# The first layer's gated outputs are stored through GpSimd's DMA queue instead of SyncE's

## The chip, the cores and the metric

The kernel runs on one core of a Trainium2 chip. The metric is the device time of one execution in microseconds (us), taken as the median of several runs. The engines are named as the profile names them: PE is TensorE's matmul side and PEld its weight loads, DVE is VectorE, ACT is ScalarE, POOL is GpSimd, SP is SyncE. SP computes nothing here; it only issues DMAs, one after the other, in the order of its instruction stream. SPq and POOLq are the queues of DMA issues of those engines.

## The reference, cut to what is computed

The program is one inference step of a decoder with two layers, on a prompt of 2048 positions and on a sample group of 8 sequences with 4 positions each, with the same weights. The width is 1024. The first layer is gated linear attention, with 4 heads of key width 128 and value width 512:

```python
def gla_mixer(h, state0, norm_g, w_in, w_gate2, b_gate, out_norm_g, w_out):
    u = rmsnorm(h, norm_g)
    q, k, v, gate, g_low = split(u @ w_in)
    log_a = log_sigmoid(g_low @ w_gate2 + b_gate) / 16
    o, state = gla_recurrence(q * 128 ** -0.5, k, v, log_a, state0)
    o = rmsnorm(o, out_norm_g)
    return (o * silu(gate)) @ w_out, state
```

The recurrence keeps a 128 x 512 state for each head; within a chunk, position t reads position s with a weight that decays channel by channel with the summed log_a between them. After the first layer, keys and values are projected once from the normalised residual. The second layer is attention over a window of 128 positions with sinks, with a gate path of the same kind, that reads those keys and values. The kernel returns the residual streams, the states and the last keys and values.

## The kernel before

All large matrix products run on PE in float16. Each float32 operand is split into a high and a low half, and each product is made in three passes (high by high, and two mixed ones), so PE has three times the matmuls that plain float16 would need. The helper `split` (lines 189 to 198) makes the two halves: the high half is a copy on ACT (line 194, or 197 with a scale), the low half a subtraction on POOL or DVE (line 195, or 198 with a scale).

**The first layer.** For each of the 4 heads the kernel walks over 4 blocks of 512 positions, and in each block over 4 chunks of 128. A block first projects q, k, the log gates, v and the gate path (matmuls into the PSUM tile `pj`, whose inputs are the weights `W` and the transposed, normalised input `uT`). It then makes the decayed scores by levels (lines 500 to 536): for each level POOL (line 508) and DVE (line 509) form differences of summed logs in the tile `E`, ACT takes the exponential, DVE multiplies by k and q, `split` writes both halves into the tile `X` (2 buffers), PE multiplies into `lev`, and DVE copies what belongs to this level into the score tile `S`. A chunk (lines 562 to 616) is a list of steps: `kv` (state update product), `out` (readout into `o`), `upd` (the new state and its halves), `norm` (ACT squares and sums, POOL takes the power in lines 186 and 187, DVE multiplies the readout by the norm and the gate into the tile `og`, 1 buffer), and last `spill_og`.

**The touched step.** `spill_og` (lines 620 to 623) takes a buffer of `ogT` (128 x 2 x 512 float16, 2 buffers), splits `og` into it, high half on ACT (line 194), low half on POOL (line 195), and stores it to the DRAM tensor `ogd` with one DMA of 256 KB (line 623). The trace has 68 of these stores. They are read back much later, when the output projection of the first layer runs. `ogT` also carries the normalised input of each 128 positions until it is transposed: `norm_T` (lines 300 to 322) uses `og` as scratch for the squares (lines 302 and 307), writes the halves into `ogT` (lines 197 and 198), and SP issues the transposing DMAs to `uT` (line 322).

**What else SP and POOL do there.** SP loads the inputs (line 382), the constants (line 108), the raw weights, the rope tables (line 894 into the tile `pst`, 2 buffers) and issues the transposing DMA of `ke` (line 558). POOL multiplies the rope tables by the norm's gains (lines 897, or 899 and 900), stores them (line 901, its own DMA queue, tensor `rtd`), and later prepares the weights of the next products: `prepare` splits them into `pst` and stores them from POOL's queue (line 248, tensor `pre`, 72 stores).

**What sets the order.** The program is written as lists of steps with priorities (`behind`), woven together. A scheduler then fixes the order of instructions on each engine, from a timeline of its own at build time. So a changed instruction can move others. On the chip each engine runs its stream in order, and waits on semaphores where an operand or a buffer is not ready. An instruction that waits holds up all that stands behind it on its engine; that includes DMA issues on SP and on POOL.

Of the kernel before, what the change touches and what calls it, by code (L numbers as in the profile page):

```python
# [74 lines left out]
def _body(tc, nc, cp, sb, ps, dr, i, o):  # L75
# [6 lines left out]
    def T(tag, shape, dt, bufs=None):  # L82
        return sb.tile(shape, dt, tag=tag, name=nm(tag), **({} if bufs is None else {"bufs": bufs}))
# [106 lines left out]
    def split(dst, src, sc=None, eng=dve):  # L190

        hi, lo = dst
        if sc is None:
            act(hi, src, AF.Copy)  # L194
            eng.tensor_tensor(lo, src, hi, ALU.subtract)  # L195
        else:
            act(hi, src, AF.Copy, scale=sc)  # L197
            dve.scalar_tensor_tensor(lo, src, sc, hi, ALU.mult, ALU.subtract)  # L198
# [217 lines left out]
    class Blk:  # L416
# [149 lines left out]
        def chunk_steps(self, c):  # L566
# [40 lines left out]
            def norm():  # L607
# [6 lines left out]
                dve.scalar_tensor_tensor(og, po, r[:, 0:1], self.sg[c], ALU.mult, ALU.mult)  # L614

            return behind([kv, out, upd, norm], -20) + [lambda: spill_og(box["og"], ogd[j * 4 + c], h, pool)]

    state = [None]

    def spill_og(og, dst, h, eng):  # L620
        ot = T("ogT", [P, 2, 512], F16, 2)
        split((ot[:, 0], ot[:, 1]), og, eng=eng)
        nc.sync.dma_start(dst[:, :, h * 512 : (h + 1) * 512], ot)

    def spill_halves(og, c, g):

# [1217 lines left out]
```

## Time and profile before

| what | value |
|---|---|
| median of 3 runs | 2862.65 us |
| the three runs | 2855.01, 2862.65, 2867.41 us |
| the profiled execution's own time | 2863.85 us |
| its span (first to last instruction) | 2862.1 us |
| mean granted clock of PE over the span | 0.983 |
| PE busy | 2735.9 us, 96% of the span |
| DVE, ACT, POOL busy | 1845.7, 1440.3, 1063.6 us |

The profiled execution took 1.75 us more than its span, and 1.2 us more than the median of the runs. The first layer's blocks run from about 100 us to 1180 us: the 68 stores of line 623 begin at 106.5 us and end at 1160.2 us. Before that lie the first loads and the first transposes, behind it the output projection of the first layer, the shared keys and values, and the second layer. Busy time of an engine counts instructions that compute; an issue of a DMA has a duration in the trace too, but is not counted as busy.

### The profile page before, as it was taken

How to read it: one execution, taken by the hardware profiler on the slowest of the kernel's cores; microseconds unless marked ns; L12 is line 12 of the kernel's file. 1: busy time of each engine (PE TensorE's matmuls, PEld its weight loads, DVE VectorE, ACT ScalarE, POOL GpSimd, SP SyncE). 2: the span in 40 equal slices, each digit the busy share in tenths (PEclk: the TensorE clock that was granted, in tenths of full speed). 3: DMA queues.
4: the chain of work that ended last, by engine and by line, in shares of the span. 5: the costliest groups of instructions: out<-in, count | busy, mean ns of one | idle time of the engine just before them, and what ended most of it. 6: DMA issues, size and time to landing. Idle time of an engine off the chain costs nothing.

```text
span 2862.1 us, 51609 instructions
## 1 busy us (share of the span) xinstructions
PE 2735.9 (96%) x19070; PEld 1392.4 (49%) x19070; DVE 1845.7 (64%) x3815; ACT 1440.3 (50%) x3385; POOL 1063.6 (37%) x1471
## 2 busy tenths in 40 slices
PE   6899999999999999999899999999999999988999
PEld 3445444444454444444344555555555555543444
DVE  5767787677768775336413666677777766767653
ACT  6655665466546654333313555566666666641110
POOL 1242233222322321116405676666566556530000
PEclk9899999999999999999999999999999999999999
DMA  8351334124312533799975555866877788798651
GB/s 209 90 124 36 100 101 150 38 82 136 115 38 85 171 84 96 180 240 282 233 193 135 108 130 120 203 117 129 173 116 130 157 155 165 151 236 172 125 112 57
DMA packets 774230, 391.78 MB, mean 137 GB/s; under 512 B 629200, under 2 KB 698776, under 8 KB 773944
## 3 DMA queue, kind: packets, MB, share of 16 engines
q1 hardware_dynamic: 761016, 352.75, 54.6%
q0 software_dynamic: 10880, 35.66, 3.4%
q8 instruction: 149, 2.44, 0.4%
q14 instruction: 105, 0.86, 0.1%
q10 hardware_dynamic: 2080, 0.07, 0.0%
HBM read 138.90 MB, written 107.54 MB: 86 GB/s over the span
## 4 chain that ended last, share of the span: by engine, by line
PE 56%; DVE 12%; DMA 11%; ACT 10%; issue 6%; POOL 4%; SPq 1%; DVEq 0%; ACTq 0%; POOLq 0%
PE pj L101 33%; PE o L101 11%; PE tr L101 8%; PE kv L101 3%; ACT o L1279 2%; DMA pst<-v 2%; DVE v L198 2%; ACT v L197 2%; DMA pre<-pst 1%; PE lev L101 1%; DMA wraw<-in_a_w_in_dram 1%; DVE o L1274 1%; DVE W L198 1%; POOL ogT L195 1%; DVE lev L1274 1%
## 5 line engine op out<-in xcount | busy, mean ns | idle before, releaser
L101 PE MATMUL pj<-W,uT 128*128 128x512 f16 x5088 | 1208.1, 383 | 6.6 <-ACT qT L430 2.9
L101 PEld LDWEIGHTS <-uT 128*128 128x128 f16 x6976 | 654.7, 99 | 714.1 <-issue 40.4
L101 PE MATMUL tr<-W,uT 128*128 128x512 f16 x1536 | 365.8, 379 | 0.0
L186 POOL TENSOR_SCALAR rs_m<-ss 128x1 f32<-128x1 f32 (+3 forms) x190 | 46.1, 243 | 685.7 <-ACT og L611 234.0
L101 PEld LDWEIGHTS <-X 128*128 128x128 f16 x2744 | 185.8, 98 | 149.3 <-issue 14.7
L1279 ACT ACTIVATE o<-o,mx 128x256 f32<-128x256 f32 (+1 forms) x384 | 168.5, 439 | 168.1 <-DVE mx L1274 163.6
L1274 DVE CUSTOM_DVE_ANT_0 o<-o,madd,nsink 128x256 f32<-128x256 f32 (+1 forms) x384 | 184.0, 479 | 48.3 <-PE o L101 44.0
L101 PE MATMUL pj<-uT,W 128*128 128x512 f16 (+1 forms) x912 | 186.0, 354 | 27.0 <-DMA uT<-ogT 24.3
L198 DVE SCALAR_TENSOR_TENSOR v<-o,v 128x512 f16<-128x512 f32 (+1 forms) x192 | 128.8, 671 | 102.0 <-ACT v L197 82.0
L187 POOL TENSOR_TENSOR rs_r<-rs_m,mhalf 128x1 f32<-128x1 f32 (+2 forms) x186 | 184.8, 994 | 14.4
L101 PEld LDWEIGHTS <-W 128*128 128x128 f16 x2448 | 128.0, 98 | 113.1 <-issue 18.5
L101 PEld LDWEIGHTS <-v 128*128 128x128 f16 x976 | 95.2, 98 | 116.0 <-DMA v<-ogd 1.9
L508 POOL TENSOR_TENSOR E<-bt 128x256 f32<-128x256 f32 x96 | 73.9, 770 | 198.4 <-DVE X L195 124.8
L195 POOL TENSOR_TENSOR ogT<-og,ogT 128x512 f16<-128x512 f32 x68 | 88.0, 1295 | 154.4 <-ACT ogT L194 142.5
L101 PEld LDWEIGHTS <-sth 128*128 128x128 f16 x2080 | 111.4, 99 | 52.3 <-DMA sth<-v 12.2
L101 PEld LDWEIGHTS <-sg 128*128 128x128 f16 x800 | 78.6, 99 | 107.5 <-DMA sg<-ogd 12.3
L101 PE MATMUL o<-gl,X 128*128 128x256 f16 (+1 forms) x768 | 114.9, 273 | 5.5 <-DMA X<-qe 5.5
L197 ACT ACTIVATE v<-o 128x512 f16<-128x512 f32 (+1 forms) x192 | 111.3, 579 | 11.1 <-DMA sth<-v 7.6
L101 PE MATMUL kv<-rmask,sth 128*128 128x64 f16 x1984 | 107.0, 194 | 10.1 <-DMA sth<-v 9.2
L101 PE MATMUL kv<-rmask,pst 128*128 128x64 f16 x992 | 102.4, 194 | 9.3 <-DMA pst<-v 9.3
L1279 ACT ACTIVATE lev<-lev,mx 128x256 f32<-128x256 f32 (+1 forms) x128 | 56.5, 441 | 103.3 <-DVE mx L1274 101.2
L101 PE MATMUL pj<-W,v 128*128 128x512 f16 x448 | 104.2, 379 | 1.1 <-DMA v<-ogd 1.1
(468 smaller groups left out, 5092.5 us busy)
## 6 DMA issues: line engine op xcount, KB each, us to landing
pre<-pst POOLq DMA_DIRECT2D x72, 256.0 KB, 3.4
W<-pre SPq DMA_DIRECT2D x36, 512.0 KB
ogd<-ogT SPq DMA_DIRECT2D x68, 256.0 KB
wraw<-in_a_w_in_dram SPq DMA_DIRECT2D x64, 256.0 KB
wraw<-in_b_w_in_dram SPq DMA_DIRECT2D x64, 256.0 KB
oge<-ogT SPq DMA_DIRECT2D x64, 256.0 KB
wraw<-in_a_w_out_dram SPq DMA_DIRECT2D x32, 256.0 KB
X<-in_x_prompt_dram SPq DMA_DIRECT2D x32, 256.0 KB
```

Of the source, the lines that this page charges most:

```text
L101: return order(nc.tensor.matmul(*a, **k))
L186: pool.tensor_scalar(m[:n, :k], ss, a, b, ALU.mult, ALU.add)
L187: pool.tensor_tensor(r[:n, :k], m[:n, :k], mhalf[:n, :k], ALU.pow)
L195: eng.tensor_tensor(lo, src, hi, ALU.subtract)
L197: act(hi, src, AF.Copy, scale=sc)
L198: dve.scalar_tensor_tensor(lo, src, sc, hi, ALU.mult, ALU.subtract)
L508: pool.tensor_tensor(Ev[:, :, 0, :], ref, btv[:, :, 0, :], ALU.subtract)
L1274: dve.tensor_tensor_reduce(pm[:, z], pm[:, z], madd.rearrange("p a b -> p (a b)")[:, (2 - nk) * P :], -0.125, nsink[:, g * GRP + h : g * G ...
L1279: act(pm[:, z], pm[:, z], AF.Exp, scale=-1.0, bias=nm_[:, h : h + 1], accum_out=bx["sum"][:, h : h + 1])
```

## The change

One line changes: the store at the end of `spill_og` is issued by GpSimd's queue.

```diff
     def spill_og(og, dst, h, eng):
         ot = T("ogT", [P, 2, 512], F16, 2)
         split((ot[:, 0], ot[:, 1]), og, eng=eng)
-        nc.sync.dma_start(dst[:, :, h * 512 : (h + 1) * 512], ot)
+        nc.gpsimd.dma_start(dst[:, :, h * 512 : (h + 1) * 512], ot)
```

Over the program SP's stream loses 68 rows (1448 to 1380) and POOL's gains 68 (1469 to 1537). On POOL each store stands directly behind the subtraction of line 195 that fills its buffer, at some places with one small instruction between. The scheduler also reorders neighbours in the first layer. PE, DVE and ACT keep the same instructions; on PE the order differs at places up to about a third of the stream, and is the same from there to the end.

On SP, in the stretch in which the constants of line 108 are loaded (from about 137 us in the trace of before), one stretch of the difference reads as follows; `W_1974` is a piece of the input, `ogd_99` the store of one chunk, `gso` and `gskv` are the first two of the constants.

```order
 L322 DMA_TRANSPOSE uT_158<-ogT_1460 128x8x128
 L322 DMA_TRANSPOSE uT_158<-ogT_1461 128x8x128
-L382 DMA W_1974<-in_x_prompt_dram 128x512 x2
-L623 DMA ogd_99<-ogT_1513 256x1x512
 L108 DMA gso<-in_a_out_norm_dram 128x4x1
 L108 DMA gskv<-in_kv_norm_dram 128x8x1
```

The constants follow directly on the transposes; the load of `W_1974` stands further down now, between two of the last constants (`bmq` and `smask`), and another store (`ogd_100`) that stood ahead of the first rope load is gone from SP as well.

On POOL, at the rope tables (from about 159 us in the trace of before), where `pst_2857` and `pst_2865` are the third and fourth table, `rtd` their stores, and `ogT_1860` the buffer of the chunk whose store is `ogd_101`, the difference reads:

```order
-L901 DMA rtd<-pst_2673 128x8x64
-L195 TENSOR_TENSOR ogT_1860<-og_1849,ogT_1860 128x512
 L899 TENSOR_TENSOR pst_2857<-pst_2857,gq 128x8x32
 L900 TENSOR_TENSOR pst_2857<-pst_2857,gq 128x8x32
+L899 TENSOR_TENSOR pst_2865<-pst_2865,gq 128x8x32
+L900 TENSOR_TENSOR pst_2865<-pst_2865,gq 128x8x32
+L195 TENSOR_TENSOR ogT_1860<-og_1849,ogT_1860 128x512
+L901 DMA rtd<-pst_2857 128x8x64
+L901 DMA rtd<-pst_2865 128x8x64
+L623 DMA ogd_101<-ogT_1860 256x1x512
 L186 TENSOR_SCALAR rs_m_1959<-ss_1955 128x1
```

The subtraction that fills `ogT_1860` stood ahead of the third table's multiplications and now stands behind those of the third and fourth; its store comes after the two stores of the tables.

On PE, a little later (at about 179 us in the trace of before), the first product of a block's diagonal level, `lev_1879`, stands among the projections `pj_2050` of another block. In the difference its surroundings read:

```order
+L101 MATMUL pj_2050<-W_701,uT_157 128x512
+L101 LDWEIGHTS uT_157
+L101 MATMUL pj_2050<-W_701,uT_157 128x512
 L101 LDWEIGHTS X_1876
 L101 MATMUL lev_1879<-one_h,X_1876 128x1
 L101 LDWEIGHTS uT_157
-L101 MATMUL pj_2050<-W_692,uT_157 128x512
-L101 LDWEIGHTS uT_157
-L101 MATMUL pj_2050<-W_692,uT_157 128x512
```

Nine of the projection matmuls that stood behind `lev_1879` now stand ahead of it. Elsewhere on PE the level products move ahead of at most 8 such matmuls.

## Rows read from the trace of the kernel before

**Rows 1.** Page, part 1: busy us, share of the span, instructions of each engine

```profile
PE 2735.9 (96%) x19070; PEld 1392.4 (49%) x19070; DVE 1845.7 (64%) x3815; ACT 1440.3 (50%) x3385; POOL 1063.6 (37%) x1471
```

**Rows 2.** Windows: stretch, length, busy PE, PEld, DVE, ACT, POOL, clock, DMA share, GB/s

```profile
140.00:230.00 90.00, 83.17 (x468) 39.39 (x467) 63.34 (x115) 53.05 (x103) 34.84 (x48) 0.97 0.49 118
230.00:1180.00 950.00, 927.40 (x5887) 446.99 (x5886) 682.06 (x1217) 540.84 (x1004) 240.83 (x355) 0.99 0.33 99
```

**Rows 3.** Waits of SP's queue, whole span: total us, times, longest us

```profile
SPq L623 <- POOL ogT L195: 262.0, 40, 22.1
```

**Rows 4.** Waits of PE: first two lines 100 to 230 us, others 230 to 1180

```profile
PE pj L101 <- DMA uT<-ogT: 1.7, 1, 1.7
...
PE kv L101 <- DMA ke<-X: 0.8, 1, 0.8
...
PE lev L101 <- ACT ssm L194: 5.8, 3, 2.5
PE kv L101 <- ACT v L197: 4.6, 4, 1.8
PE kv L101 <- DVE v L198: 3.9, 4, 2.4
...
PE o L101 <- DVE ke L774: 0.5, 1, 0.5
```

**Rows 5.** Line 623: ns min/median/max of an issue, first and last start

```profile
L623 SPq DMA_DIRECT2D ogd<-ogT x68: 533/546/1201, 106.5 to 1160.2; - x68
```

**Rows 6.** Line 248 on POOL, the same view, and its landing times

```profile
L248 POOL DMA_DIRECT2D pre<-pst x72: 677/690/785, 414.0 to 1283.8; - x72
...
DMA to landing us min/median/max: 2.5/3.4/6.1
```

**Rows 7.** Timeline of POOL behind line 195: start us, us, instruction, [idle before <- releaser]

```profile
107.75 0.61 POOL L508 TENSOR_TENSOR E<-bt 128x256 f32<-128x256 f32 x1 [1.30 <-DVE X L195]
...
140.42 0.18 POOL L544 COPY ebl<-E 128x4 f32<-128x4 f32 x1
...
1153.57 0.63 POOL L878 DMA_DIRECT2D wf<-Sh  x1
...
1164.19 0.72 POOL L248 DMA_DIRECT2D pre<-pst  x1 [4.16 <-DVE pst L198]
```

**Rows 8.** Timeline of SP and DVE, 124 to 130 us

```profile
124.71 0.58 SPq L623 DMA_DIRECT2D ogd<-ogT  x1
129.25 0.75 DVE L198 SCALAR_TENSOR_TENSOR ogT<-W,rs_r,ogT 128x512 f16<-128x512 f32 x1 [0.31 <-ACT ogT L197]
129.86 2.62 SPq L322 DMA_TRANSPOSE uT<-ogT  x2
```

**Rows 9.** Timeline of SP, 137 to 165 us

```profile
137.36 1.36 SPq L382 DMA_DIRECT2D W<-in_x_prompt_dram  x2
...
141.10 1.35 SPq L108 DMA_DIRECT2D gso<-in_a_out_norm_dram  x1
...
155.30 10.06 SPq L894 DMA_DIRECT2D pst<-in_c_rope_dram  x3
```

**Rows 10.** Timeline of POOL, 158 to 174 us

```profile
158.95 1.26 POOL L897 TENSOR_TENSOR pst<-pst,gq 128x512 f32<-128x512 f32 x1 [12.99 <-DMA pst<-in_c_rope_dram]
...
164.79 1.15 POOL L195 TENSOR_TENSOR ogT<-og,ogT 128x512 f16<-128x512 f32 x1 [0.66 <-ACT ogT L194]
...
172.35 1.18 POOL L900 TENSOR_TENSOR pst<-pst,gq 128x256 f32<-128x256 f32 x1
```

**Rows 11.** Timeline of ACT and PE, 165 to 180 us

```profile
165.97 0.63 ACT L302 ACTIVATE og<-W 128x512 bf16<-128x512 f32 x1
...
172.77 2.54 PE L101 MATMUL pj<-W,uT 128*128 128x512 f16 x11
179.02 0.18 PE L101 MATMUL lev<-one_h,X 128*128 128x1 f16 x1 [3.71 <-ACT X L197]
```

**Rows 12.** Windows, as in rows 2, of the ten us behind that wait

```profile
180.00:190.00 10.00, 10.00 (x46) 4.33 (x45) 10.00 (x14) 4.48 (x8) 7.02 (x7) 0.83 1.05 229
```

## The prediction

> **What bounds the kernel now.** I read the page's busy times first. PE is busy 2735.9 us, 96% of the span [rows 1], so a change of 68 DMA issues can move the end only where PE waits. The stores run from 106.5 to 1160.2 us [rows 5]; behind them the order of every engine that computes is the old one. So I read the first layer in windows. From 230 to 1180 us PE is busy 927.4 of 950 us [rows 2]: 22.6 us idle. The waits of PE say what it waited for there: nine lines, the largest 5.8 us, the last 0.5 us, all of them ACT or DVE, no DMA [rows 4]. Then the queue of SP: it waited 262.0 us in 40 places with a store of line 623 at its head, for POOL's subtraction [rows 3]. That is the number that makes the change look large; but nobody on PE's side waits for SP in those 950 us. From 140 to 230 us PE is busy 83.17 of 90 us [rows 2]. This stretch is the exception: the constants and rope tables pass through SP in it, and the waits of PE from 100 to 230 us have two short ones that end with a DMA, 1.7 and 0.8 us [rows 4].
>
> **The change, part by part.**
>
> *SP loses the stores.* 68 issues at 0.546 us [rows 5] are 37.1 us of SP's time, and the 262.0 us of waiting at the head of its queue go too. The transfers that came late behind them are hidden by PE's 927.4 us of work. Where PE waited for a DMA, 1.7 + 0.8 = 2.5 us [rows 4], is the most that this part can give directly. The transposes of this stretch do not wait for a store: the pair issued at 129.86 us follows DVE's half at 129.25 us, 5 us behind the store at 124.71 us [rows 8]. So I take 0, with 2.5 us as the lower end.
>
> *The constants and rope tables come earlier.* In the new order of SP the constants follow on the transposes, where the input load and a store stood: they begin at 137.36 instead of 141.10 us [rows 9], 3.74 us earlier. The input load of 1.36 us [rows 9] now stands among them, and one more store of 0.546 us is gone ahead of the rope loads: 3.74 − 1.36 + 0.55 = 2.9 us earlier for the loads at 155.30 us [rows 9], if the ring of `pst` does not hold them back.
>
> *POOL's subtraction for `ogT_1860` goes behind the second pair of tables.* In the trace it ran at 164.79 us; the second pair's last multiplication ended at 172.35 + 1.18 = 173.53 us [rows 10]. With the tables 2.9 us earlier that is 170.6 us, so the subtraction comes 5.8 us later. `og` has one buffer, so the squares on ACT that used it at 165.97 us [rows 11] come behind it, and with them, in ACT's order, the exponentials and the copy into `X` on which PE waited 3.71 us at 179.02 us [rows 11]. The new order of PE puts nine projections ahead of that product; eleven took 2.54 us [rows 11], so nine take 2.1 us and cover as much. The upper end is 5.8 − 2.1 = +3.7 us. The lower end is that earlier tables and the new order of ACT make the wait vanish, −3.7 us, and with it the lower clock behind it: the granted clock from 180 to 190 us is 0.83 [rows 12], a mean between the level of 2.4 and that of 1.2 GHz, and at full level these ten us would be 10 × 0.17 = 1.7 us shorter. The two ends lie nearly alike around nothing; I take 0.
>
> *POOL issues the stores.* No store of 256 KB from this tile on POOL is in the trace; the nearest row is line 248, the same size on the same queue, 690 ns with 677 and 785 as ends [rows 6]. 68 × 0.69 = 46.9 us, on an engine that is busy 240.83 of 950 us in the stretch [rows 2]. What counts is what stands behind the store: after 48 of the 68 subtractions POOL's next instruction came after a gap of 0.62 us or more, as the first of them, 1.30 us, and the last, 4.16 us [rows 7]; there the store fits in the gap but for a tenth. After 20 the next followed at once or nearly (first the copy at 140.42, last the store at 1153.57 us [rows 7]), so 20 × 0.69 = 13.8 us are pushed on to others, the upper end. How much arrives at PE? DVE idles 950 − 682.06 = 267.9 us in the stretch and PE 22.6 us [rows 2]: of the delays that DVE feels, 22.6 / 267.9 = 0.084 shows on PE. 13.8 × 0.084 = +1.2 us is an estimate by that ratio, and I take it.
>
> *The buffers of `ogT`.* The two are shared with the normalised input, and a store from POOL has to land before its buffer is refilled. Line 248's stores land after 3.4 us at the median, 6.1 us at most [rows 6]. At the tightest place the buffer stored at 124.71 us was refilled at 129.25 us [rows 8], 4.54 us later. At the median there is no wait, at the maximum 6.1 − 4.54 = 1.6 us. I take 0; upper end +1.6 us.
>
> *The sample group's products.* The largest wait of the stretch is 5.8 us for the halves `ssm` [rows 4]; some of its inputs move earlier in the new order. Lower end −5.8 us, taken 0.
>
> Sum: 2863.85 us (the profiled execution's own time) + 1.2 = 2865.05 us. That execution is 1.2 us over the median of the runs, 2862.65 us, so as a median the forecast is **2863.9 us**. About 0.5%, 14.3 us, is what a measurement of this kernel can tell from no change; this is well inside it.
>
> **The rivals.**
>
> *SP's relief reaches PE.* If the waits at the store's head were what made DVE and ACT late, through inputs and rope tables, PE's waits shrink: 3.7 + 1.7 + 2.5 + 5.8 = 13.7 us by the lower ends above, and the two waits of `kv` for `v`, 4.6 + 3.9 us [rows 4], on top: 22.2 us, 2862.65 − 22.2 = 2840.4 us. For it speaks the size of 262.0 us [rows 3]; against it that these waits of PE name evictions on ACT and DVE, which take their input from PSUM. Chance 0.07.
>
> *POOL takes SP's place as the queue that is held up.* The place is the 20 subtractions with work right behind them. POOL works for the levels (line 508) and for the norm's power, both ahead of DVE and ACT; if PE's lead on these chains is thinner than its idle time says, all of 13.8 us arrives, with 1.6 us of the ring and 3.7 us at the rope tables: 2862.65 + 19.1 = 2881.8 us. It decides once a delay of 0.69 us is longer than the lead that DVE's results have over PE at those places. For it: waits of PE that name ACT and DVE exist, 4.6 and 3.9 us [rows 4]. Against it: PE is 98% busy in the stretch. Chance 0.09.
>
> *The store waits for DVE.* An issue on POOL might be held until the DVE instruction beside it ends, one of 0.75 us [rows 8]: 0.69 + 0.75 = 1.44 us each, 20 × 1.44 = 28.8 us, 2862.65 + 28.8 = 2891.5 us if all of it arrives. Against it: 72 issues of line 248 lie between 677 and 785 ns, while DVE is busy 682.06 of 950 us [rows 2, 6]; a wait of that size would be seen among them. Chance 0.03.
> The Trainium skill, in "SBUF — State Buffer", section "SBUF: two separate sides", has such a rule: a DMA issued from GpSimd's queue cannot have its descriptors written while VectorE runs an operation that takes both ports, and it advises SyncE's or ScalarE's queue instead. By it this change would be a loss; the narrow spread of line 248 does not bear it out here.
>
> That the stores do not move at all is excluded, since all 68 stand on POOL in the new order.
>
> **How the numbers follow.** The forecast has 0.81, the rivals 0.07, 0.09 and 0.03. The forecast's own range: below, all lower ends, 2862.65 − 13.7 = 2849 us; above, half of POOL's 13.8 with the ring's 1.6 and the rope tables' 3.7 us, 2862.65 + 12.2 = 2875 us, and one us more for the spread of a median. 2849 to 2876 us leaves out the rivals, 0.19. Faster by over 0.5% (under 2848.3 us) is the first rival, 0.07; slower (over 2877 us) the two others, 0.12; within 0.81.
>
> **What would show it.** In the profile of the changed kernel: line 623 on POOL at about 0.69 us and landing at about 3.4 us; no wait of SP's queue for line 195 any more; the first multiplication of a rope table about 2.9 us earlier than 158.95 us; the subtraction of `ogT_1860` near 170 us, and a wait of PE near 179 us of 0 to 7 us; PE idle between 22 and 25 us from 230 to 1180 us. PE idle of 35 us or more there would speak for POOL as the new queue that is held up; idle under 15 us for SP's relief; issues of line 623 over 1 us for the wait on DVE. The prediction is wrong if the span changes by more than 14 us, or if the second layer, whose order is the same, changes by more than a few.

## The result and the profile after

The changed kernel takes 2867.68 us, the kernel before 2862.02 us (medians of 22 runs each): a ratio of 1.002 with a 95% interval of 1.001 to 1.0029. That is 5.7 us, 0.2%, slower. The forecast was 2863.9 us, with 2849 to 2876 us as its range, and "no change within 0.5%" as the likeliest case. A second series with the same program, beside new runs of the kernel before, gave 1.0008, 0.9996 to 1.0019. So the cost is between nothing and 0.3%, and it is less than the 0.5% that the forecast called no change.

The profiled execution of the changed kernel took 2869.98 us, its span is 2868.2 us. The first line of the page after, busy time of each engine, answers to [rows 1]:

```profile
PE 2730.7 (95%) x19070; PEld 1391.1 (49%) x19070; DVE 1849.8 (64%) x3815; ACT 1439.0 (50%) x3385; POOL 1111.5 (39%) x1539
```

POOL is 47.9 us busier, and has 68 more instructions. So, other than was said of busy time ahead of the prediction, the page counts issues on POOL as busy time, and 68 stores at 0.73 us are 50 us. The windows of after, with the columns of [rows 2]:

```profile
140.00:230.00 90.00, 85.00 (x485) 40.71 (x484) 64.31 (x120) 53.01 (x104) 38.60 (x53) 0.98 0.49 121
230.00:1180.00 950.00, 922.07 (x5870) 444.75 (x5867) 685.58 (x1220) 539.99 (x1000) 282.98 (x414) 0.99 0.33 99
```

From 140 to 230 us PE idles 5.0 us where it idled 6.8; from 230 to 1180 us it idles 27.9 us where it idled 22.6. One stretch got better and the other worse.

The waits of SP's queue in after (total us, times, longest) no longer have line 623. Other entries of the same queue have grown instead; the second was 61.2 us in 4 places before:

```profile
SPq L223 <- DVE W L198: 195.3, 57, 26.4
SPq L558 <- DVE E L370: 183.4, 7, 59.1
```

Added up over all lines of this view, SP's queue waited 906 us from 100 to 1180 us before and 948 us after. So most of the 262.0 us of [rows 3] did not become earlier transfers. The next entry of the queue waits in place of the store.

Line 623 of after (ns min/median/max of one issue, first and last start; then what POOL stood idle for ahead of it, us and times; then its landing) answers to [rows 5] and [rows 6]:

```profile
L623 POOL DMA_DIRECT2D ogd<-ogT x68: 682/734/860, 106.1 to 1160.3; - x68
...
  POOL ogT L195: 14.0, 47
...
DMA to landing us min/median/max: 2.5/2.6/7.7
```

The second row matters most for what follows. 47 of the stores stood idle for 14.0 us in all, 0.30 us each, until the subtraction just ahead of them on the same engine was signalled as done. Such a store costs POOL 0.73 + 0.30 = 1.03 us, not 0.69 us.

The waits of PE in after, 230 to 1180 us, answer to the last four of [rows 4]:

```profile
PE kv L101 <- ACT v L197: 6.3, 5, 2.5
PE kv L101 <- DVE v L198: 5.3, 5, 2.4
PE o L101 <- DVE ke L774: 3.1, 3, 1.3
...
PE lev L101 <- ACT ssm L194: 1.1, 1, 1.1
```

The wait for `ssm` fell from 5.8 to 1.1 us, and those for evictions on ACT and DVE grew. None of them is a DMA.

The place of the constants and rope tables in after: SP, POOL, and then PE, as in [rows 9] to [rows 11]:

```profile
136.82 0.57 SPq L108 DMA_DIRECT2D gso<-in_a_out_norm_dram  x1
...
149.88 20.64 SPq L894 DMA_DIRECT2D pst<-in_c_rope_dram  x6
...
153.00 2.48 POOL L897 TENSOR_TENSOR pst<-pst,gq 128x512 f32<-128x512 f32 x2 [5.29 <-DMA pst<-in_c_rope_dram]
...
161.47 0.72 POOL L899 TENSOR_TENSOR pst<-pst,gq 128x256 f32<-128x256 f32 x1 [0.34 <-DMA pst<-in_c_rope_dram]
...
164.20 1.16 POOL L195 TENSOR_TENSOR ogT<-og,ogT 128x512 f16<-128x512 f32 x1
...
169.62 7.29 PE L101 MATMUL pj<-W,uT 128*128 128x512 f16 x33
176.74 0.17 PE L101 MATMUL lev<-one_h,X 128*128 128x1 f16 x1
```

The constants begin 4.3 us earlier, the rope loads 5.4 us, the first multiplication 6.0 us. The subtraction of `ogT_1860` runs at 164.20 us, no later than before. PE reaches the product `lev` without a wait, where it waited 3.71 us. The granted clock of PE from 180 to 185 us was 0.66 before, a mean of its two levels (1.2 and 2.4 GHz), behind that wait. Here it is 1.00, the upper level; in the second trace of the changed kernel, without that wait, it is 0.66 again.

### The profile page after: what moved, and what is told of

Same layout as the page of the kernel before. It is cut to its first block, busy times and chain, and to the rows that moved or that the text cites. A ratio compares the mean times of both kernels' runs of the same rounds, so it can differ in the third digit from the quotient of the medians.

```text
span 2868.2 us, 51585 instructions
## 1 busy us (share of the span) xinstructions
PE 2730.7 (95%) x19070; PEld 1391.1 (49%) x19070; DVE 1849.8 (64%) x3815; ACT 1439.0 (50%) x3385; POOL 1111.5 (39%) x1539
## 4 chain that ended last, share of the span: by engine, by line
PE 56%; DVE 11%; DMA 10%; ACT 10%; issue 6%; POOL 4%; SPq 1%; DVEq 0%; ACTq 0%; POOLq 0%
PE pj L101 33%; PE o L101 10%; PE tr L101 8%; PE kv L101 3%; ACT o L1279 2%; DVE v L198 2%; ACT v L197 2%; DMA pst<-v 2%; DMA pre<-pst 2%; PE lev L101 1%; DVE o L1274 1%; DMA wraw<-in_a_w_in_dram 1%; DVE lev L1274 1%; DMA uT<-ogT 1%; DVE pst L198 1%
## 5 line engine op out<-in xcount | busy, mean ns | idle before, releaser
L101 PE MATMUL kv<-rmask,sth 128*128 128x64 f16 x1984 | 107.6, 195 | 13.1 <-DMA sth<-v 12.2
```

Of the source, the lines that this page charges most:

```text
L101: return order(nc.tensor.matmul(*a, **k))
```

## The experiments

**How the stretches are measured.** All kernels here have 19070 matmuls. In each trace I took their starts in order of time, and the length of three stretches: from the 800th to the 1200th (about 156 to 235 us, the constants and rope tables), from the 1200th to the 7200th (to about 1210 us, the rest of the first layer), and from there to the last. The order of PE's stream is nearly the same in all, so the nth matmul is the same work but for a few neighbours. The last column is behind all stores.

| kernel | time by that of before, run beside it (95%) | 800 to 1200, us | 1200 to 7200, us | 7200 to end, us |
|---|---|---|---|---|
| before | 1 | 78.9 | 974.9 | 1647.8 |
| before_again | one run | 79.6 | 973.9 | 1651.1 |
| after | 1.002 (1.001 to 1.0029) | 75.2 | 977.8 | 1655.3 |
| after_again | 1.0008 (0.9996 to 1.0019) | 76.4 | 979.3 | 1645.3 |
| queue_alone | 1.0005 (0.9995 to 1.0016) | 75.8 | 977.7 | 1648.2 |
| order_alone | 1.0016 (1.0002 to 1.003) | 82.0 | 973.9 | 1643.1 |
| first5_pool | 0.9987 (0.9977 to 0.9997) | 75.0 | 971.7 | 1645.4 |
| late_pool | 1.0027 (1.0015 to 1.004) | 78.3 | 976.5 | 1643.7 |
| issue_alone | 1.0008 (0.9999 to 1.0017) | 78.4 | 976.4 | 1646.9 |
| two_issues | 1.0066 (1.0054 to 1.0078) | 76.0 | 991.6 | 1650.6 |
| covered_pool | 0.9997 (0.9988 to 1.0005) | 78.4 | 972.2 | 1647.7 |
| uncovered_pool | 1.0012 (1.0003 to 1.0021) | 79.4 | 980.2 | 1646.3 |
| deferred_pool | 0.9995 (0.9982 to 1.0007) | 75.1 | 969.6 | 1656.4 |
| loads_first | 0.999 (0.9979 to 1.0001) | 75.5 | 974.9 | 1644.8 |

The two traces of the kernel before differ by 0.7, 1.0 and 3.3 us in the three stretches, those of the changed kernel by 1.2, 1.5 and 10.0 us. In the first column all kernels with the early stores on SP and in the order of before lie between 78.3 and 79.6 us, and all without the two stores ahead of the constants between 75.0 and 76.4 us, so a step of 3 us says something there. In the second column the four kernels with all stores on SP in that stretch and no DMA added (before, before_again, order_alone, loads_first) lie between 973.9 and 974.9 us. But first5_pool, which has no moved store in that stretch either, lies at 971.7 us; so a step of 2 to 3 us is not clear of scatter there. In the third column no step below 10 us says anything.

**How the order is held.** The scheduler changes the order on each engine when the store moves. To tell the queue from the order, a table at the end of the program fixes the place of each instruction on its engine with edges that order without a wait. All kernels but after_again and before_again carry it, besides the line that they change:

```diff
+    traced = {x.name: x for x in nc.cur_bb.bb.instructions}
+    for engine, steps in json.loads(zlib.decompress(base64.b64decode(PLACES))):
+        names = sorted((n for n, x in traced.items() if place_of(x) == engine and int(n[2:]) not in FREE), key=lambda n: int(n[2:]))
+        at, before = -1, None
...
+        for step in steps:
+            at += step + 1
+            if before is not None:
+                tc.add_manual_dep(traced[names[at]], before, mybir.DependencyInfo(mybir.DependencyClass.NoSync, mybir.DependencyReason.DATA), reason="place")
+            before = names[at]
```

### The queue and the order apart

queue_alone has the changed line and the order of before on all engines; POOL's stores stand right behind their subtractions.

```diff
-        nc.sync.dma_start(dst[:, :, h * 512 : (h + 1) * 512], ot)
+        nc.gpsimd.dma_start(dst[:, :, h * 512 : (h + 1) * 512], ot)
```

> The stores go to POOL, each right behind its subtraction, and every other instruction keeps the order of the kernel before (a table fixes it). Theory 1, the issues on POOL cost and the new order is worth little: 4 to 8 us slower than before. Theory 2, the new order costs and the queue does not: within 2 us of before. Theory 3, the loss arises behind 1180 us, where transfers meet each other at other times, whatever moved them: 3 to 7 us slower, with PE's matmuls level with before until about 1330 us and late from there.

order_alone keeps the line as before and has only the table, here with the order of the changed kernel; the 68 stores are not in it and are left to the scheduler on SP.

> The stores stay on SP, and PE, DVE, ACT and POOL have the order of the changed kernel (a table fixes it; SP's other instructions too). Theory 1: 3 us faster to 1 us slower than before, with 3 to 4 us gained by 235 us, where PE no longer waits 3.7 us. Theory 2: 4 to 8 us slower. Theory 3: 3 to 7 us slower, the loss behind 1330 us.

after_again and before_again are the two programs unchanged.

> The changed kernel once more, on this chip and with a second trace. All theories: 4 to 7 us slower than before. If the steps of its trace are its own, the lead by about 235 us is 3 to 5 us again and the loss behind 1330 us again 5 to 8 us; if they are chance, the steps fall elsewhere.

> The kernel before once more, for a second trace. If the waits at 1370 to 1410 us are fixed by the program, PE goes on at 1384 us within 1 us; the difference of two traces of the same program is the floor below which a step says nothing: expected under 2 us anywhere.

queue_alone shows both effects without any reordering: 3 to 4 us won between the 800th and the 1200th matmul, and 3 to 4 us lost between the 1200th and the 7200th. Its time is that of before within the interval. The expectation of a clear loss of 4 to 8 us for theory 1 was not met, since that theory had only the loss in it. order_alone wins nothing in the first stretch, it loses 2 to 3 us there, and it is level in the second. So the nine projections that the new order puts ahead of `lev` [rows 11] did not cause the lead, and the 3 to 4 us that theory 1 expected of the order were not there. Its runs are 0.16% slower than before, with an interval that starts at 0.02%. Its trace shows where the first stretch loses: with the stores on SP the rope tables come late, the subtraction of `ogT_1860` comes behind the second pair of them, and ACT's squares wait for it. POOL and ACT in order_alone:

```profile
170.48 1.15 POOL L195 TENSOR_TENSOR ogT<-og,ogT 128x512 f16<-128x512 f32 x1
...
171.67 0.63 ACT L302 ACTIVATE og<-W 128x512 bf16<-128x512 f32 x1 [6.11 <-POOL ogT L195]
```

Before, the two stood at 164.79 and 165.97 us [rows 10, 11]. PE in queue_alone, with the old order:

```profile
169.48 5.34 PE L101 MATMUL pj<-W,uT 128*128 128x512 f16 x24
174.66 0.17 PE L101 MATMUL lev<-one_h,X 128*128 128x1 f16 x1
```

There is no idle time ahead of `lev`, with no projections added. POOL and ACT behind the first rope table, in the trace of before, whose first multiplication ran at 158.95 us [rows 10], and then in queue_alone:

```profile
162.69 0.57 POOL L187 TENSOR_TENSOR rs_r<-rs_m,mhalf 128x1 f32<-128x1 f32 x1
...
164.07 0.63 ACT L194 ACTIVATE ogT<-og 128x512 f16<-128x512 f32 x1 [3.03 <-DVE og L614]
```

```profile
154.83 1.26 POOL L897 TENSOR_TENSOR pst<-pst,gq 128x512 f32<-128x512 f32 x1 [7.91 <-DMA pst<-in_c_rope_dram]
...
158.41 0.58 POOL L187 TENSOR_TENSOR rs_r<-rs_m,mhalf 128x1 f32<-128x1 f32 x1
...
160.45 0.62 ACT L194 ACTIVATE ogT<-og 128x512 f16<-128x512 f32 x1
```

The power of the norm (line 187) stands on POOL behind the first tables' multiplications, which wait for a load that SP issued late. DVE's multiplication by that norm waits for the power, and ACT's copy of `og` waits for DVE, 3.03 us before and not at all in queue_alone. This is the path by which SP's lateness came to PE, whose wait names only ACT. In the seven kernels of the order of before in which PE waits at `lev` (the six with the early stores on SP, and loads_first below), `lev` starts 19.7 to 20.2 us behind the first multiplication, whenever that was. This much is read from the traces; the runs below show that the lead starts at SP.

The third theory, a loss behind 1180 us in all moved kernels, is not borne out: behind the 7200th matmul the changed kernel took 7.5 us more than before in its first trace and 2.5 us less in its second, and order_alone 4.7 us less. before_again was to stay within 2 us of before at any matmul; it was up to 5.7 us away, so that floor was set too low. Nor did PE go on at 1384 us within 1 us, it did at 1381.0 us. after_again had the expected lead by 235 us, but its time, 1.5 us over before by the medians, misses the 4 to 7 us that all theories had, and it has not the loss behind 1330 us: that step of the first trace did not come again.

### The early stores and the late ones

first5_pool moves only the first five stores, to about 166 us; late_pool the other 63. Both have the order of before.

```diff
-    def spill_og(og, dst, h, eng):
+    def spill_og(og, dst, h, eng, stored=[]):
...
-        nc.sync.dma_start(dst[:, :, h * 512 : (h + 1) * 512], ot)
+        stored.append(1); (nc.gpsimd if len(stored) <= 5 else nc.sync).dma_start(dst[:, :, h * 512 : (h + 1) * 512], ot)
```

late_pool has `len(stored) > 5` there.

> Only the first five stores (to about 166 us) go to POOL; all else keeps the order of before. Theory, SP's relief at the constants and rope tables gains and the later issues on POOL cost: a lead of 3 to 5 us from about 235 us, kept to 1210 us, and 2 to 5 us faster than before if the stage behind 1330 us doesn't take it back. Rival, the lead comes from elsewhere (all 68 stores are needed): no lead at 235 us, within 1 us of before. Rival, a lead is always taken back where PE waits for the read of the stored outputs at about 1384 us: lead at 1210 us, none behind it.

> The other 63 stores go to POOL, the first five stay on SP; order of before. Theory: no lead at 235 us, 3 to 5 us lost between 235 and 1210 us, 2 to 6 us slower in all. Rival: a lead at 235 us also here, and within 1 us of before.

first5_pool has the whole lead, keeps it, and is 0.13% faster than before (2855.39 against 2859.55 us). late_pool has no lead and is 0.27% slower; it is the largest loss but for two_issues. The two effects have opposite signs and separate places; by the medians 4.2 us won and 7.8 us lost (2867.31 against 2859.55 us) leave 3.6 us, between the changed kernel's two series. late_pool's trace shows less, 976.5 − 974.4 = 2.1 us in the second stretch (974.4 is the mean of the two traces of before); it is of the fastest of its runs (2860.92 us), as first5_pool's is (2850.97 us). The 7.8 us lie above the 2 to 6 us expected, and the 2.1 us below the 3 to 5, so how much the late stores cost is not settled by this pair.

loads_first keeps all stores on SP. It only takes the third and fourth from ahead of the constants and rope loads and puts them behind the first two rope loads (the edges that hold each constant behind the entry ahead of it on SP, line 108, are dropped, since the table holds the order, and those two places are changed in the table).

```diff
-        tc.keep_in_program_order(q.dma_start(dst, src))
+        q.dma_start(dst, src)
```

> All stores on SP; the third and fourth no longer stand ahead of the constants and the rope tables on SP but behind the first two rope loads, all else as before. Theory, SP's relief there makes the lead: the stretch from the 800th to the 1200th matmul takes 75 to 77 us, not 78.3 to 80, and the kernel is 1.5 to 4 us faster than before. Rival, the lead is POOL's doing: 78 to 80 us and no change.

The stretch from the 800th to the 1200th matmul took 75.5 us, as with the stores on POOL. SP, POOL and PE in this kernel:

```profile
135.76 0.44 SPq L108 DMA_DIRECT2D gso<-in_a_out_norm_dram  x1
...
149.48 1.01 SPq L894 DMA_DIRECT2D pst<-in_c_rope_dram  x2
150.58 1.23 SPq L623 DMA_DIRECT2D ogd<-ogT  x2
...
152.71 1.26 POOL L897 TENSOR_TENSOR pst<-pst,gq 128x512 f32<-128x512 f32 x1 [9.30 <-DMA pst<-in_c_rope_dram]
...
161.53 0.73 POOL L899 TENSOR_TENSOR pst<-pst,gq 128x256 f32<-128x256 f32 x1 [1.83 <-DMA pst<-in_c_rope_dram]
...
164.68 0.73 POOL L899 TENSOR_TENSOR pst<-pst,gq 128x256 f32<-128x256 f32 x1 [1.46 <-DMA pst<-in_c_rope_dram]
...
172.50 0.18 PE L101 MATMUL lev<-one_h,X 128*128 128x1 f16 x1 [0.42 <-ACT X L197]
```

So the lead is SP's relief and not POOL's doing: two stores stood ahead of loads that POOL waits for. Of the two only the first held SP up by waiting, 1.8 us for POOL's subtraction (SP was idle from 138.72 to 140.50 us before); the other cost its issue of 0.54 us. POOL still waits for the third and fourth table, 1.83 and 1.46 us, about as before; these waits moved with the whole chain, and the lead does not come from them. By its time the kernel is 0.999 of before, with an interval that just reaches 1.

### What a store costs on POOL

issue_alone leaves the stores on SP and adds one small DMA on POOL behind each subtraction, without touching `ogT`. two_issues adds it behind each store of queue_alone.

```diff
+    extra = {a: nc.gpsimd.dma_start(dr.tile([P, 16], F32, tag=f"xt{a}", name=f"xt{a}"), mhalf).ins for a in AFTER}
...
+            if before in extra:
+                tc.add_manual_dep(extra[before], before, mybir.DependencyInfo(mybir.DependencyClass.NoSync, mybir.DependencyReason.DATA), reason="place")
+                before = extra[before].name
```

> All stores stay on SP; behind each of the 68 subtractions POOL issues one more DMA, of 8 KB from a constant to a scratch tensor, at 0.5 to 0.8 us each. Theory, POOL's time for the issue is what costs: 3 to 5 us lost between 235 and 1210 us and no lead before. Rival, the cost is in the store itself (its landing, the buffers of ogT): under 1.5 us lost.

> As queue_alone, with the extra 8 KB DMA behind each store: POOL's issue time doubles. Theory: lead at 235 us as in queue_alone, 3 to 5 us; the loss between 235 and 1210 us doubles to 6 to 9 us. If the gaps of POOL are used up by the first issue, all of the second arrives: up to 30 us lost. Rival: loss as in queue_alone, 3 to 5 us.

issue_alone lost 976.4 − 974.4 = 2.0 us in the second stretch, less than the 3 to 5 us expected, more than the rival's 1.5 us, and within what traces scatter. It does not decide by itself. two_issues shows more: the second issue on POOL added 991.6 − 977.7 = 13.9 us, four times what the first did, 17 us in all where 6 to 9 were expected of a doubling. The same 68 extra DMAs cost 2.0 us where no store stood ahead of them, so it is not their transfers. The window of 230 to 1180 us in two_issues:

```profile
230.00:1180.00 950.00, 913.51 (x5822) 439.50 (x5820) 679.11 (x1209) 534.96 (x994) 319.07 (x472) 0.99 0.33 98
```

PE idles 36.5 us there, and POOL is still only 34% busy. The cost does not go with POOL's load. The reading that fits is that it goes with how much of the work behind the issue is pushed beyond its gap. In the trace of before, counted over the 63 late stores, the time by which POOL's next instruction followed the subtraction too soon is 23.6 us for a store of 1.03 us and 49.0 us for store and second DMA of 1.7 us. Of the first, some 3.5 us reached PE (15%), of the second 17 us (35%). That a larger share arrives the further a chain is pushed would fit, but it is not shown: of the 19.6 us that belong to the 19 stores of uncovered_pool below, 30% arrives.

covered_pool moves the 44 late stores that had a gap of 0.62 us or more behind them, uncovered_pool the 19 that had none.

```diff
...
-        nc.sync.dma_start(dst[:, :, h * 512 : (h + 1) * 512], ot)
+        stored.append(1); (nc.gpsimd if len(stored) in MOVED else nc.sync).dma_start(dst[:, :, h * 512 : (h + 1) * 512], ot)
```

> Of the 63 later stores, the 44 behind whose subtraction POOL stood idle for 0.62 us or more in the trace of before go to POOL; the other 24 stay on SP; order of before. The stretch from the 1200th to the 7200th matmul takes 974 to 975 us in the kernel before and 978 us with all stores on POOL. Theory, only what stands directly behind the store pays: 974 to 975.5 us. Rival, each store costs 0.73 us and the 0.30 us for which it waits on the subtraction, so gaps under 1.03 us don't cover it: 9 us of POOL's time are uncovered, 975 to 976.5 us. Rival, the cost is spread over all stores: 976 to 977 us.

> The other 19 of the 63 go to POOL, those with POOL's next instruction right behind the subtraction; order of before. Theory: 976.5 to 978 us for the same stretch, the whole loss with 19 of 63 stores. Rival, gaps under 1.03 us count as well: 975.5 to 977 us. Rival, spread: 975 to 976 us.

The two lie 8.0 us apart: with the 44 covered stores moved the stretch takes 972.2 us, 2.2 us below before, with the 19 uncovered ones 980.2 us, 980.2 − 974.4 = 5.8 us above it. The times agree: the medians of their runs are 2859.37 and 2863.27 us, and 2858.64 us for the kernel before beside them. Both stretches lie outside the range that the theory gave, one below and one above, by 2 us, which is what scatter can do. 5.8 us is a little more than the full set costs; covered and uncovered together, −2.2 + 5.8 = +3.6 us, come near the 3.3 us of queue_alone. In covered_pool each store still waits the 0.30 us for its subtraction, 13.1 us over 44:

```profile
L623 POOL DMA_DIRECT2D ogd<-ogT x44: 682/726/739, 188.9 to 1158.0; - x44
...
  POOL ogT L195: 13.1, 44
```

That gaps under 1.03 us do not cover a store, the first rival, is not seen, though 18 of the 44 had less. But it could hardly be seen: by the trace of before these 18 leave 4.0 us of POOL's time uncovered, not the 9 us of the expectation, and at the share of 15 to 30% that is about 1 us at PE. An uncovered store in uncovered_pool:

```profile
1153.61 1.20 POOL L195 TENSOR_TENSOR ogT<-og,ogT 128x512 f16<-128x512 f32 x1 [4.17 <-ACT ogT L194]
1155.11 0.73 POOL L623 DMA_DIRECT2D ogd<-ogT  x1 [0.30 <-POOL ogT L195]
1155.76 0.66 POOL L878 DMA_DIRECT2D wf<-Sh  x1
```

What stood at 1153.57 us behind the subtraction [rows 7] now comes after the store's 0.30 + 0.73 us.

deferred_pool has all 68 on POOL, each behind those of POOL's instructions that follow at once, at the first gap of 1.1 us or more in the trace of before; the table holds these places.

```diff
...
-        nc.sync.dma_start(dst[:, :, h * 512 : (h + 1) * 512], ot)
+        stored.append(1); (nc.gpsimd if len(stored) in MOVED else nc.sync).dma_start(dst[:, :, h * 512 : (h + 1) * 512], ot)
```

`MOVED` holds all 68 here.

> All 68 stores on POOL, but each stands behind those of POOL's next instructions that follow at once, at the first gap of 1.1 us or more in the trace of before; order of before on the other engines. Theory, the cost is what the store holds up on POOL: lead of 3 to 4 us at 235 us as in queue_alone, and 974 to 975.5 us for the stretch; 2 to 5 us faster than before in all. Rival, the cost is the landing on the buffers of ogT: 977 to 979 us or more, since the stores come later.

The second stretch took 969.6 us, the shortest of all, with the lead of the first stretch besides: the loss of queue_alone is gone. It is 4 to 5 us below before, but only 2.1 us below first5_pool, so a gain in this stretch is not shown. Its buffers of `ogT` are held longer than in queue_alone, so the landing was not the cost. In its trace the stage behind the 7200th matmul took 1656.4 us, the longest, and the runs give 0.9995 with an interval that holds both 3.4 us won (the difference of the medians) and no change. Whether that stage takes the lead back for a reason, or by chance as in the first trace of the changed kernel, is open.

## Why the prediction was right, point by point

The forecast was nearly no change, with +1.2 us as its sum. That came out in part by luck: two of its terms, taken as 0 and +1.2 us, were about −3.3 and +4 us, and they cancel.

**The bound.** A change of 68 issues can move the end only where PE waits, and those waits are for ACT and DVE. This held: none of the waits of PE from 230 to 1180 us in the changed kernel is a DMA, and no kernel here but two_issues moved by more than 0.3%.

**SP loses the stores.** Taken as 0. As a part of the whole span this held: SP's queue waits elsewhere now. covered_pool and deferred_pool are 2 to 5 us below before in the second stretch, but so is first5_pool, by 2.7 us, with every store of that stretch on SP; so a gain from it there is not shown.

**The constants and rope tables.** The step that failed in size. The forecast set the earlier tables against a subtraction that comes 5.8 us later, with ends of −3.7 and +3.7 us, and took the middle. What happened is the lower end: about −3.3 us (78.8 us as the mean of the six kernels with the early stores on SP and in the order of before; 75.6 us for the seven without the two stores ahead of the constants). The loads came 5.4 us earlier, not 2.9 us, and the third table with them, so the subtraction stayed at 164 us. The mistake was to shift POOL's second pair of tables by SP's issue times alone; their wait was for the load, which came earlier still. The upper end was real too: in order_alone, where the loads stay late, the subtraction ran at 170.48 us, as forecast (near 170 us), ACT's squares came 5.7 us later, and the stretch lost 3.2 us against the same mean, near the +3.7 us of the upper end.

**POOL issues the stores.** The mechanism was right, the term was too small: +1.2 us was forecast, about +4 us measured (978.3 us as the mean of three traces with all stores on POOL right behind their subtractions, 974.2 us of the three with all on SP and no store shifted). PE's idle time from 230 to 1180 us, 27.9 us, lies above the 22 to 25 us of the forecast and below the 35 us of its rival. Two parts of its working were off. An issue took 0.73 us and not 0.69, as a landing took 2.6 us and not 3.4, which changes little; but the store also waits 0.30 us for its subtraction, which line 248 does not show, since its input comes from other engines. Line 901, which stores what POOL itself has written, showed it in the trace of before, 0.30 us in 4 of its 8 stores:

```profile
181.31 0.95 POOL L901 DMA_DIRECT2D rtd<-pst  x1 [0.30 <-POOL pst L897]
```

That was the nearer row. And the ratio of PE's to DVE's idle time, 0.084, was no measure of what arrives: of 23.6 us by which gaps were overrun, 15% did, and of the 19.6 us of uncovered_pool 30%. The list of what stands behind the 20 uncovered stores was the right thing to read; uncovered_pool shows that the 19 of them behind 166 us hold the loss.

**The buffers of `ogT`.** Taken as 0: no row of the changed kernel shows a wait for the landing of one of these stores on a buffer of `ogT`.

**The sample group's products.** Taken as 0, with −5.8 us as an end. The wait did shrink by 4.7 us, and others grew by as much; order_alone, with the same new order, is level in that stretch. queue_alone, in the order of before, has 9.1 us of this wait.

**The rivals.** SP's relief reached PE, but for 3 us and in one place. POOL as the queue that is held up did as well, for 4 us where all of it would have been 19. Each was the other's cover. The third, a store that waits for DVE, did not happen: the issues lie between 682 and 860 ns, with DVE busy 685.58 of 950 us. The Trainium skill, in "SBUF — State Buffer", section "SBUF: two separate sides", warns that a GpSimd DMA is starved of descriptors while VectorE holds the shared port. In these 68 stores nothing of the kind is seen, with a median landing of 2.6 us; how often DVE's instructions here hold that port no row shows.

**What stays open.** The first two stretches of the changed kernel add up to nothing: 1053.0 and 1055.7 us against 1053.8 and 1053.5 us. So its loss of 5.7 us in one series and about 2 us in the other (0.0008 of the time) is either chance in the stage behind them, whose length differs by 10 us between two traces of the same program, or a small effect there that one trace of each kernel cannot show.

## What to carry to other kernels

A small verdict can hide two real effects: look for a lead and a loss by the starts of the same matmul in both traces, then move half of the change. In an in-order queue what counts is what stands behind an entry, both where it is taken away (two stores ahead of loads that another engine waits for: 3 us) and where it is put (19 of 63 places with work right behind them held the whole loss). The one version here whose interval lies wholly below 1 moves only the first five stores, 0.13% faster than the kernel before; loads_first, which keeps all on SP, has the same 4 us by the medians, and the two cannot be told apart.

## What the runs showed of the hardware

A DMA on POOL's queue that stores what POOL has just written stood idle for 0.30 us until that instruction was signalled as done, 47 times of 68 in the changed kernel; the issue then took 0.73 us. An 8 KB DMA from a constant took nearly as long to issue (620 to 667 ns in two_issues) as the 256 KB store (731 ns at the median there). The landing of the stores was faster than that of line 248 on the same queue, 2.6 against 3.5 us at the median in the changed kernel.
